# Two groups of heads ahead of the second query block, and a rank 300 ahead for the heads' work, in a two-layer trunk

## The chip, the cores and the metric

The kernel runs on one core of one Trainium2 chip. The core has TensorE (PE in the profile, with its weight loads shown apart as PEld), VectorE (DVE), ScalarE (ACT), GpSimd (POOL) and SyncE (SP), which here issues nearly all DMAs. The metric is device time in microseconds, the median of several runs. One execution of the kernel is profiled.

## The reference

Two layers work on x of 256 rows by 1024 columns in fp32, each as x = x + mixer(rms_norm(x)).

```python
# layer 0 (nsa): 16 query heads in 4 groups g, one key/value head per group
q, kc, vc, ks, vs, kw, vw, gl, z = split(h @ w_in)
q = rope(rms_norm(q));  k_cmp, v_cmp = compress(kc), compress(vc)   # 15 blocks of 32 rows
o = gate0 * attend(q, k_cmp, v_cmp) + gate1 * attend(q, ks, vs) + gate2 * attend(q, kw, vw)
x = x + (o * silu(z)) @ w_out
# layer 1 (swa with sinks): 16 query heads, 2 key/value heads, window of 128
q, k, v, z = split(h @ w_in);  q, k = rope(rms_norm(q)), rope(rms_norm(k))
x = x + (attend(q, k, v, window=128, sink) * silu(z)) @ w_out
```

Every attention needs the queries of its heads, the keys, a masked softmax over at most 256 keys, and at its end the gate silu(z) of its heads.

## The kernel before

The 256 rows are two halves of 128 (h = 0 and 1). The 16 heads are four groups of four, numbered g or u. Every projection works on weights that are loaded in fp32 (`wraw`), copied by ScalarE to a high part (`wh`, line 147) and split by VectorE into a low part (`wl`, line 175), so that each product takes three matmuls. `wraw`, `wh` and `wl` have five buffers each.

Each layer is written as a list of steps. `q0` and `q1` (`queries`, `queries1`) project the queries of heads 0 to 7 and 8 to 15: 48 matmuls 512 columns wide for each, into the two PSUM banks with the tag `acc`. Then `q_prep` applies the rotary factors (VectorE, lines 316 and 317, and GpSimd, line 66), splits the result (`qs`) and transposes it on TensorE into PSUM tiles `ptq` (line 343), which ScalarE copies to `qT`. `z0` to `z3` (`z_gate`) project the gate of one group: 48 matmuls of 256 columns into the one bank `pz`, which VectorE reads out in line 393 (`zt`). `a0` to `a3` (`attend0`, `attend1`) are the heads of one group, for both halves: score matmuls into `s` or `sb` (two banks), scores to `p` on VectorE (line 407), the exponential on ScalarE (line 409), the scaling of `p`, its transposes into `ptp` (line 440) and of the small compressed part into `ptcs` (line 770), the product with the values into `po` (one bank), and `finish_unit`, which multiplies by `zt` and splits the result into `oz` for `out_proj`. `a0` and `a1` need the queries of `q0`, `a2` and `a3` those of `q1`. `out_proj` sums into `pya` (tag `acc`), `pyb` (tag `s`) and, in layer 1, `tail`. `ptn`, `ptk`, `ptq`, `ptp` and `ptcs` share two PSUM banks with the tag `pt`.

The order on each engine is set when the kernel is built, by a scheduler that plays the program through with costs of its own. Among the instructions whose inputs and buffers are ready it takes the one with the lowest rank. An instruction's rank is its place in the written order, and `tc.high_priority(offset=n)` ranks what is inside it n places ahead: 200 for the weight splits (`HP`) and for the read-out of the gate (`HPZ`), 250 for `q_prep` (`HPQ`) and `k_prep` (`HPK`), 100 for the copies out of `ptp` (`HPT`). The heads' work has no offset of its own. Once built, each engine runs its own list in order.

Of the kernel before, what the change touches and what calls it, by code (L numbers as in the profile page):

```python
# [33 lines left out]
EPS = 1e-6  # L34
NEG = -1e30
HP, HPZ, HPS, HPT, HPQ, HPF = 200, 200, 0, 100, 250, 0
HPC, HPK, NWARM2 = 300, 250, 4
RSC, QLO = 'p', 'd'
WPS = ('d', 'd', 'd', 'd', 'd', 'd', 'd', 'd', 'd')
PHASES = (4, 13, 23, 29, 37, 43, 49, 55)  # L40
# [50 lines left out]
def tile_hybrid_trunk(ctx: ExitStack, tc: tile.TileContext, x, positions, norm_gains, a_w_in, a_cmp_pos,  # L91
# [18 lines left out]
    def banks(name, tag="acc"):  # L110
        return [bank(f"{name}{h}", tag) for h in range(2)]
# [66 lines left out]
    def load_w(w, k0, nk, c0, n):  # L178
        return split_w(load_raw(w, k0, nk, c0, n))
# [112 lines left out]
    def proj(acc, hT, h, w, nk, k0):  # L292

        wh, wl = w
        for k in range(nk):
            hh = hT[:, 0, k0 + k, h * 128:(h + 1) * 128]
            hl = hT[:, 1, k0 + k, h * 128:(h + 1) * 128]
            for i, (s, m) in enumerate(((hh, wh), (hh, wl), (hl, wh))):
                mm(acc, s, m[:, k, :], k0 + k == 0 and i == 0, k0 + k == 7 and i == 2)
# [23 lines left out]
    def heads(ap):  # L323
        return ap.rearrange("p (n d) -> p n d", d=HD)
# [458 lines left out]
            finish_unit(po, zt, h, g, oz)  # L783


    for step in 'q0 z0 a0 q1 z1 a1 z2 a2 z3 a3'.split():
        {'q': queries, 'z': zs0, 'a': attend0}[step[0]](int(step[1:]))


    sqs = work.tile([128, 2, 2], F32, name="sqs1", tag="sqs")  # L790
# [25 lines left out]
    def keys1():  # L816
        acc = banks("akv1", "s")
        wk = [load_w(bwi, k0, 4, 1024, 256) for k0 in (0, 4)]
        for kk in range(2):
            for h in range(2):  # L820
                proj(acc[h][:, 0:256], hT, h, wk[kk], 4, 4 * kk)
        k_prep([heads(acc[h][:, 0:128]) for h in range(2)], 2, 5, kt1, (0, 128), r1)
        for h in range(2):
            nc.scalar.activation(v1[:, h], heads(acc[h][:, 128:256]), AF.Copy, scale=r1[:, h:h + 1])
# [40 lines left out]
            pv(po, [(v1[:, b, g, :], transpose_p([ps[i][:, b] for i in range(4)])) for b in range(nb)], True)  # L865
            finish_unit(po, zt, h, u, oz)

    for step in 'q0 k0 z0 a0 q1 z1 a1 z2 a2 z3 a3'.split():
        {'q': queries1, 'k': lambda n: keys1(), 'z': zs1, 'a': attend1}[step[0]](int(step[1:]))
    out_proj(ozs, bwo, xh, None, True)  # L870


# [31 lines left out]
```

## Time and profile before

| | us |
|---|---|
| median of 3 runs | 289.81 |
| lowest and highest run | 289.19, 290.7 |
| the profiled execution, its own time | 289.28 |
| its span, first to last instruction | 287.6 |
| TensorE busy in the span | 272.4 |
| VectorE busy in the span | 217.6 |
| ScalarE busy in the span | 189.4 |
| GpSimd busy in the span | 124.9 |

The span is what the trace covers. The execution's own time is 1.68 us longer, which lies around the span. TensorE's busy time is the time in which at least one matmul is shown as running.

### The profile page before, as it was taken

The numbers are of one execution on the slowest core, as the hardware profiler recorded it, in microseconds if no ns is written. First come the engines' busy times: TensorE is split into PE (matmuls) and PEld (weight loads), VectorE is DVE, ScalarE is ACT, GpSimd is POOL, SyncE is SP. The second block draws the span as 40 slices with busy tenths as digits, with TensorE's granted clock in tenths as the row PEclk, the third lists the DMA queues.
The fourth block names the chain that finished last, engine by engine and source line by source line (L and its number), as shares of the span: only waits on it lengthen the run. The fifth ranks groups of instructions, "written<-read, shape, count | busy, mean of one in ns | idle before, by whom it ended". The sixth has DMA issues, their size and how long they took to land.

```text
span 287.6 us, 5296 instructions
## 1 busy us (share of the span) xinstructions
PE 272.4 (95%) x1780; PEld 232.3 (81%) x1780; DVE 217.6 (76%) x579; ACT 189.4 (66%) x457; POOL 124.9 (43%) x188
## 2 busy tenths in 40 slices
PE   6989999999999799988998999999999799999995
PEld 5858988888989698866776877889989699877874
DVE  3768646999979989969698374859969988784533
ACT  5694991755664758779688474757866949783620
POOL 7489308193552391726252500112694392253200
PEclk9999999999999989999999999999999989999999
DMA  7997845546474334310102345227774423100003
GB/s 224 321 293 244 310 141 146 151 143 166 130 217 146 121 106 140 86 66 13 64 0 76 146 137 159 59 87 217 217 226 148 145 77 106 43 0 0 2 0 146
DMA packets 33114, 37.51 MB, mean 130 GB/s; under 512 B 1680, under 2 KB 21568, under 8 KB 32960
## 3 DMA queue, kind: packets, MB, share of 16 engines
q1 hardware_dynamic: 33088, 37.18, 42.2%
q8 instruction: 14, 0.23, 0.3%
q14 instruction: 12, 0.10, 0.1%
HBM read 36.13 MB, written 1.05 MB: 129 GB/s over the span
## 4 chain that ended last, share of the span: by engine, by line
PE 80%; DVE 12%; ACT 4%; issue 1%; DMA 1%; SPq 0%; ACTq 0%
PE pz L114 13%; PE aqb L114 8%; PE po L114 8%; PE pya L114 7%; PE aq L114 7%; PE pyb L114 7%; PE ptp L440 4%; PE aks L114 4%; DVE wl L175 3%; PE akc L114 3%; PE avw L114 2%; PE s L114 2%; PE sb L114 2%; PE akw L114 2%; PE akv L114 2%; DVE p L407 2%
## 5 line engine op out<-in xcount | busy, mean ns | idle before, releaser
L175 DVE TENSOR_TENSOR wl<-wraw,wh 128x1024 fp32r<-128x1024 f32 (+2 forms) x64 | 80.5, 1261 | 11.2 <-ACT wh L147 10.7
L147 ACT ACTIVATE wh<-wraw 128x1024 fp32r<-128x1024 f32 (+3 forms) x58 | 59.6, 1031 | 26.3 <-issue 5.0
L114 PE MATMUL pz<-hT,wh 128*128 128x256 f32 x256 | 51.4, 296 | 2.0 <-DVE zt L393 2.0
L114 PEld LDWEIGHTS pz<-hT,wh 128*128 128x128 f32 x256 | 42.7, 200 | 2.6 <-DVE zt L393 2.0
L71 POOL TENSOR_SCALAR p<-p,rg 128x256 f32<-128x256 f32 (+1 forms) x48 | 24.1, 522 | 32.1 <-DVE rg L763 16.8
L114 PE MATMUL pz<-hT,wl 128*128 128x256 f32 x128 | 37.5, 293 | 0.0
L66 POOL TENSOR_TENSOR rt<-rt,rt 128x512 f32<-128x512 f32 (+2 forms) x14 | 19.1, 1369 | 42.4 <-DVE rt L317 34.5
L409 ACT ACTIVATE p<-p,nm 128x128 f32<-128x128 f32 (+1 forms) x64 | 28.3, 446 | 3.7 <-DVE nm L407 3.5
L147 ACT ACTIVATE ptsb<-ptp 128x512 f32<-128x512 f32 x36 | 20.5, 586 | 10.4 <-PE ptp L440 10.4
L114 PEld LDWEIGHTS pz<-hT,wl 128*128 128x128 f32 x128 | 25.6, 200 | 0.0
L407 DVE CUSTOM_DVE_ANT_0 p<-s,mask,nrq 128x128 f32<-128x128 f32 (+1 forms) x64 | 24.2, 408 | 0.1
L114 PE MATMUL s<-kt,qT 128*128 128x272 f32 (+1 forms) x96 | 19.8, 306 | 1.8 <-DVE cwide L736 0.7
L114 PE MATMUL aqb<-wh,hT 128*128 128x512 f32 x64 | 21.4, 397 | 0.0
L114 PE MATMUL aq<-wh,hT 128*128 128x512 f32 x64 | 20.9, 395 | 0.0
L71 POOL TENSOR_SCALAR pb<-pb,rg 128x128 f32<-128x128 f32 (+1 forms) x24 | 13.8, 590 | 15.5 <-DVE rg L860 9.8
L407 DVE CUSTOM_DVE_ANT_0 pb<-sb,mask,nsink 128x128 f32<-128x128 f32 (+1 forms) x32 | 13.9, 471 | 5.1 <-PE ptp L440 3.9
L114 PEld LDWEIGHTS s<-kt,qT 128*128 128x128 f32 x96 | 14.4, 190 | 3.5 <-PE s L114 1.2
L273 ACT ACTIVATE hT<-ptn,gT 128x128 fp32r<-128x128 f32 x32 | 10.8, 363 | 9.0 <-PE ptn L267 5.5
L440 PE MATMUL ptp<-identr,p 128*128 128x128 f32 x96 | 14.9, 275 | 1.8 <-ACT ptsb L147 1.8
L409 ACT ACTIVATE pb<-pb,nm 128x128 f32<-128x128 f32 (+1 forms) x32 | 14.2, 447 | 2.6 <-DVE nm L407 2.5
L114 PEld LDWEIGHTS aq<-wh,hT 128*128 128x128 f32 x64 | 12.0, 188 | 2.3
L440 PEld LDWEIGHTS ptp<-identr,p 128*128 128x128 f32 x96 | 11.2, 140 | 3.2 <-ACT ptsb L147 2.6
(246 smaller groups left out, 694.1 us busy)
## 6 DMA issues: line engine op xcount, KB each, us to landing
wraw<-in_a_w_in_dram SPq DMA_DIRECT2D x25, 512.0 KB, 4.0
wraw<-in_b_w_in_dram SPq DMA_DIRECT2D x18, 512.0 KB, 4.3
wraw<-in_a_w_out_dram SPq DMA_DIRECT2D x8, 512.0 KB, 3.6
wraw<-in_b_w_out_dram SPq DMA_DIRECT2D x8, 512.0 KB, 3.7
x<-in_x_dram SPq DMA_DIRECT2D x4, 256.0 KB, 4.5
w<-in_cmp_w_dram SPq DMA_DIRECT2D x1, 1024.0 KB, 4.8
x<-in_x_dram SPq DMA_DIRECT2D x2, 512.0 KB, 3.8
wraw<-in_a_w_in_dram SPq DMA_DIRECT2D x2, 456.0 KB, 6.6
```

Source lines behind the costliest of these rows:

```text
L66: self.eng.tensor_tensor(out, a, b, op=op)
L71: self.eng.tensor_scalar(out, a, s0, s1, op0=op0, op1=op1)
L114: nc.tensor.matmul(o, lhsT=l, rhs=r, start=start, stop=stop)
L147: nc.scalar.activation(dst, src, AF.Copy)
L175: e_.tensor_tensor(wl[:, ks], raw[:, ks], wh[:, ks].bitcast(F32), op=ALU.subtract)
L273: nc.scalar.activation(hi, pt[:, k], AF.Copy, scale=gk)
L407: nc.vector.tensor_tensor_reduce(out=p, in0=s, in1=mk, scale=nr, scalar=floor, op0=ALU.add, op1=ALU.min, accum_out=nm)
L409: nc.scalar.activation(p, p, AF.Exp, scale=-1.0, bias=nm, accum_out=total)
L440: nc.tensor.transpose(pt[:, i], s, ident)
```

## The change

A constant `HPA` of 300 is added. In both layers the step `q1` is written behind `z1 a1` instead of ahead of them, and every step `a` is run inside `tc.high_priority(offset=300)`. The steps themselves stay the same. An `a` step is some 155 instructions in layer 0 and some 85 in layer 1, a `z` step some 60, a `q` step some 100.

```diff
-HPC, HPK, NWARM2 = 300, 250, 4
+HPC, HPK, HPA, NWARM2 = 300, 250, 300, 4
...
-    for step in 'q0 z0 a0 q1 z1 a1 z2 a2 z3 a3'.split():
-        {'q': queries, 'z': zs0, 'a': attend0}[step[0]](int(step[1:]))
+    for step in 'q0 z0 a0 z1 a1 q1 z2 a2 z3 a3'.split():
+        with tc.high_priority(offset=HPA if step[0] == 'a' else 0):
+            {'q': queries, 'z': zs0, 'a': attend0}[step[0]](int(step[1:]))
...
-    for step in 'q0 k0 z0 a0 q1 z1 a1 z2 a2 z3 a3'.split():
-        {'q': queries1, 'k': lambda n: keys1(), 'z': zs1, 'a': attend1}[step[0]](int(step[1:]))
+    for step in 'q0 k0 z0 a0 z1 a1 q1 z2 a2 z3 a3'.split():
+        with tc.high_priority(offset=HPA if step[0] == 'a' else 0):
+            {'q': queries1, 'k': lambda n: keys1(), 'z': zs1, 'a': attend1}[step[0]](int(step[1:]))
```

## Rows read from the trace of the kernel before

**Rows 1.** The page: busy time and share of each engine; chain that ended last.

```profile
PE 272.4 (95%) x1780; PEld 232.3 (81%) x1780; DVE 217.6 (76%) x579; ACT 189.4 (66%) x457; POOL 124.9 (43%) x188
...
PE 80%; DVE 12%; ACT 4%; issue 1%; DMA 1%; SPq 0%; ACTq 0%
```

**Rows 2.** Busy time by stretch: PE, PEld, DVE, ACT, POOL, clock, DMA share, GB/s.

```profile
71.00:118.00 47.00, 44.80 (x317) 41.45 (x317) 42.69 (x120) 31.23 (x80) 23.16 (x23) 0.96 0.50 145
118.00:178.00 60.00, 56.21 (x372) 43.62 (x371) 42.32 (x171) 43.88 (x130) 19.49 (x40) 1.00 0.27 81
```

**Rows 3.** The same columns, for the three stretches in which TensorE loses most.

```profile
96.50:102.70 6.20, 4.21 (x21) 3.79 (x21) 6.13 (x18) 3.84 (x12) 2.67 (x3) 0.72 0.43 137
226.60:232.50 5.90, 3.92 (x20) 3.92 (x21) 5.90 (x19) 4.62 (x17) 4.80 (x5) 0.71 0.29 93
118.00:158.50 40.50, 36.97 (x265) 28.98 (x263) 32.81 (x151) 33.36 (x110) 15.83 (x32) 1.00 0.14 42
```

**Rows 4.** TensorE's waits: total us, times, longest.

```profile
PE pz L114 <- DVE zt L393: 2.0, 2, 1.8
PE sb L114 <- DVE nm L407: 2.0, 1, 2.0
...
PE avw L114 <- ACT wh L147: 1.6, 1, 1.6
```

**Rows 5.** Timeline of TensorE, layer 0 (start, duration, count at the end).

```profile
71.00 0.47 PE L114 MATMUL pz<-hT,wh 128*128 128x256 f32 x2
...
76.82 0.40 PE L114 MATMUL aq<-wh,hT 128*128 128x512 f32 x1
...
83.62 0.73 PE L114 MATMUL s<-kt,qT 128*128 128x272 f32 x4
...
99.33 0.80 PE L114 MATMUL pz<-hT,wh 128*128 128x256 f32 x2 [1.84 <-DVE zt L393]
```

**Rows 6.** Timeline of VectorE around the read-outs of `z0` and `z1`, layer 0.

```profile
76.65 1.23 DVE L175 TENSOR_TENSOR wl<-wraw,wh 128x1024 fp32r<-128x1024 f32 x1 [0.26 <-ACT wh L147]
77.79 0.68 DVE L304 TENSOR_REDUCE qssq<-sq 128x8 f32<-128x512 f32 x1
...
78.99 0.68 DVE L393 TENSOR_TENSOR zt<-pz,rrows 128x512 f32<-128x512 f32 x1
...
97.99 0.68 DVE L256 TENSOR_TENSOR qs<-rt,qs 128x512 fp32r<-128x512 f32 x1
98.59 0.68 DVE L393 TENSOR_TENSOR zt<-pz,rrows 128x512 f32<-128x512 f32 x1
```

**Rows 7.** Timeline of TensorE: transposes of `a0` and `q1`, scores and transpose of `a2`.

```profile
104.96 0.27 PE L770 MATMUL ptcs<-identr,cwide 128*128 128x128 f32 x1
...
122.01 0.60 PE L440 MATMUL ptp<-identr,p 128*128 128x128 f32 x4
...
123.20 0.54 PE L343 MATMUL ptq<-identr,qs 128*128 128x128 f32 x4 [0.35 <-ACT ptsb L147]
...
127.99 0.49 PE L114 MATMUL s<-kt,qT 128*128 128x272 f32 x2
...
140.28 0.27 PE L770 MATMUL ptcs<-identr,cwide 128*128 128x128 f32 x1
```

**Rows 8.** Timeline of layer 1: `q1`, then the wait of the scores.

```profile
206.43 0.40 PE L114 MATMUL aqb<-wh,hT 128*128 128x512 f32 x1
...
218.45 0.39 PE L114 MATMUL pz<-hT,wh 128*128 128x256 f32 x2
...
226.86 0.67 DVE L304 TENSOR_REDUCE qssq<-sq 128x8 f32<-128x512 f32 x1
...
228.58 1.66 PE L114 MATMUL sb<-kt,qTb 128*128 128x128 f32 x8 [2.02 <-DVE nm L407]
```

**Rows 9.** Timeline of TensorE, layer 1: scores of `a2`, then its first transposes.

```profile
246.43 1.11 PE L114 MATMUL sb<-kt,qTb 128*128 128x128 f32 x8
...
256.64 0.60 PE L440 MATMUL ptp<-identr,pb 128*128 128x128 f32 x4
```

## The prediction

> **What bounds the kernel now.** I read the page first. TensorE is busy for 272.4 of the 287.6 us and holds 80% of the chain that ended last; VectorE comes second with 217.6 us [rows 1]. So the end is TensorE's work plus the time in which it stands still or runs slowly, and the change can only touch the latter, since it adds and removes no instruction. Busy time by stretch then shows where that is. From the first gate matmul (71) to the end of layer 0 (178), TensorE is busy for 101.0 of 107 us, and VectorE for 42.7 of the first 47 us but 42.3 of the last 60 [rows 2]: the first part has two full engines, the second one. TensorE's own waits and a finer cut name three places [rows 3, 4].
>
> A: 96.5 to 102.7. TensorE has finished `z1`, the only gate bank still holds it, and `z2` waits 1.84 us for VectorE to read it out (line 393) [rows 5]. VectorE is behind with the split of `q1` (`qs`) [rows 6]. The granted clock of the stretch is 0.72: the matmuls after the wait run for a while at the lower of the two levels. 0.28 of 6.2 us is 1.7 us; with the 1.99 us not busy, A costs 3.7.
>
> B: 226.6 to 232.5, the same in layer 1. Scores wait 2.02 us for VectorE, which has just worked for `q1` (`qssq`) [rows 8]. 1.98 us not busy and 0.29 of 5.9 us: 3.7.
>
> C: 118 to 158.5. The gates and `q1` are used up, and while the heads wait for VectorE and ScalarE only `pya` fills in: 40.50 - 36.97 = 3.5 us [rows 3].
>
> **The change part by part.** *The rank.* By written order `q1` and `z1` stand behind `a0`, and still the weight splits (200 ahead) and `q_prep` (250) pass the heads on VectorE. The trace shows what that costs the heads: from the first score matmul of `a0` to its first `ptcs` 104.96 - 83.62 = 21.3 us pass, for `a2`, which meets fewer splits, 140.28 - 127.99 = 12.3 [rows 5, 7]. With 300 the heads of `a0` and `a1` go first on every engine, so `a0` should reach its transposes some 9 us sooner. That is no gain by itself, as TensorE has other work then. It gains where the fillers run out: with `z2`, `z3` and `pya` left for later, part of C is filled. I take 1.2 of C's 3.5 (bounds: 0, as the two engines are as full as before, and 3.5).
>
> The row of C has the weight loads busy for 28.98 of 40.50 us, 72%, against 41.45 of 47, 88%, from 71 to 118 [rows 2, 3]. The Trainium skill, "Perfetto Trace Analysis", section "Identifying the Most-Contended Engine", says that this share, not the busy time of the matmuls, tells how much room TensorE has left. By it C would hold 40.5 x (1 - 72/88) = 7.4 us in place of 3.5 (an estimate), a third of that 2.5, and the sum below would be 1.3 lower. I stay with 3.5, which the row shows as standing still.
>
> *The place of `q1`, gates.* A `z` step is 76.82 - 71.00 = 5.8 us of TensorE [rows 5]; `q1` is at most 218.45 - 206.43 = 12.0, with the transposes in it [rows 8]. Before, `q1` lies between `z0` and `z1`, so the bank has time to be read; then `z1` and `z2` collide (A). After, `q1` lies between `z1` and `z2`, and `z0` and `z1` are neighbours. In layer 0, `z0` ends at 76.8. VectorE is then inside a weight split and a `qssq` that rank ahead, until 78.4, so the read-out ends near 79.1 [rows 6], and the first weights of `q1` are split only after the two of `z1`. TensorE would stand for some 2 us, less the `ptq` of `q0`. If the clock falls too, the new stall costs 2 + 1.7 = 3.7, all of A; if it doesn't, or if a weight of `q1` is there, 0 to 2. I take a gain of 1.2 out of A (bounds 0 and 3.7). In layer 1 `q1` can start while the bank is read, since its weights are split early, and `z2` finds the bank long free. B should go with its cause, the work for `q1` ahead of the first scores; I take 2.6 (bounds 0 and 3.7), short of all because scores and splits still share VectorE.
>
> *The place of `q1`, transposes.* This is the cost. The transposes of all kinds share two PSUM banks, and the trace shows that these are handed out in written order: `qs` is ready at 98.7, ranked 250 ahead, and yet `ptq` comes at 123.20, right behind the last `ptp` of `a0` at 122.01 [rows 6, 7]. After the change `ptq` must wait for the last `ptp` of `a1`, and only then can `a2` score. So between `a1` and `a2` the heads pause: 127.99 - 123.20 = 4.8 us from the first `ptq` to the scores, and 12.3 from there to the first transpose, 17.1 in all in layer 0 [rows 7]; in layer 1, 4.8 + (256.64 - 246.43) = 15.0 [rows 9]. What hides it is `z2` and `z3`, 11.6 us, besides the products of `a1` and the scores of `a2`. Below, the cost is 0. Above, with those gates alone, or with them spent and the rest in their place, it is 17.1 - 11.6 = 5.5 and 3.4, and 1.7 each if the clock falls: 7.2 and 5.1. I take 0.5 each, near the lower end: `z1` and `q1`, 17.8 us, stand ahead of `z2` in the ring of five weight buffers, so `z2` and `z3` should still be there when `a1` ends.
>
> *Splits behind heads.* The weights of `q1` and the gates are now split after the ready work of the heads. Nothing in the trace shows TensorE short of weights during attention; the nearest row is its wait for a `wh` in the opening, 1.6 us [rows 4], and with 1.7 us of low clock 3.3 a layer. The cover is the ring of five, some 14 us of matmuls at 2.9 each (half a `z` step). I take 0.3 a layer (bounds 0 and 3.3). The DMAs of the weights go through SP in the written order of the loads; `z1`'s two now pass `q1`'s four, none is added, and the DMA share is 0.50 at most in these stretches [rows 2]: 0. The exponentials and copies on ScalarE and the scalings on GpSimd only change order, at 31.2 and 23.2 of 47 us [rows 2]: 0 while VectorE is fuller than both.
>
> Sum: -1.2 - 1.2 - 2.6 + 1.0 + 0.6 = -3.4. Against the profiled execution's 289.28 that is 285.9; the median of the runs shown is 0.53 higher, so 286.4.
>
> **The rivals.** *The pause decides (slower).* `z2` and `z3` are spent before `a1` ends, as TensorE takes whatever is ready whenever the heads wait. Then layer 0's pause costs its 7.2 in place of 0.5: 286.4 + 6.7 = 293.1. For it: stretch C begins, in the kernel before, where all four gates are through, and the last transposes of `a0` come only at 122 [rows 7]. Against it: the heads had no precedence there. It decides once the two pauses together cost more than 5.9 us (the other terms give -4.4, and 1.5 is 0.5%).
>
> *The stalls only move (same).* `z0` and `z1` stall in place of `z1` and `z2`, at the full 3.7, and in layer 1 `z2` and `z3` do so: the -1.2 and -2.6 fall away, 286.4 + 3.8 = 290.2. For it: one gate bank is left and VectorE's total stays. The Trainium skill says the same in "Perfetto Trace Analysis", section "Optimization Strategy": a gap that repeats on the engine that should be full can mean that there are too few buffers. The two waits at the gate bank agree with it; by this rule a new order gives nothing. That the ranks do little, as they only count among instructions ready at the same time, ends here too.
>
> *All three stalls go (much faster).* -3.7 - 3.7 - 3.5 + 1.6 = -9.3: 280.5. For it: the first transposes of `a0` have 9 us to win. Against it: VectorE is 91% busy up to 118.
>
> **How the numbers follow.** Chances: forecast 0.38, all stalls gone 0.10, stalls moved 0.23, pause decides 0.24, and 0.05 that it is slower still, by the pauses of both layers or by weights that come late. I predict the likeliest, 286.4, with 284 to 288.3 as its own range. To leave out no more than 2 in 10 the range reaches into the fast case and past the pause of layer 0: 282.0 to 294.0. Runs of one kernel differ by about 0.5%, which is 1.45 us. Faster: 0.38 + 0.10, and none of the third case, 0.48; same 0.23; slower 0.29.
>
> **What would show it.** In the changed profile the first `ptcs` should come by 97 instead of 104.96 and all `ptq` of `q1` behind `a1`'s last `ptp`. The 1.84 us wait between `z1` and `z2` and the one at 228 should be gone; a wait for line 393 near 77 says that A moved. At the pause I look for `pz` on TensorE between `a1`'s last `ptp` and `a2`'s first. Waits of TensorE there, or for `wh` and `wl`, with a lower clock behind them, would make the prediction wrong; so would a total busy time of TensorE that differs by more than the low clock explains.

## The result, and the profile after

The changed kernel takes 305.69 us (median of 4 runs, 305.0 to 308.9) against 290.25 for the kernel before, timed beside it: a ratio of 1.055 (1.0507 to 1.0593). The prediction was 286.4, with a range up to 294. The span of the profiled execution is 304.3 us against 287.6, so 16.7 us are to be found.

The page after, which answers to [rows 1]: no instruction has been added to TensorE, and its busy time is 8.8 us longer.

```profile
PE 281.2 (92%) x1780; PEld 235.0 (77%) x1780; DVE 218.6 (72%) x579; ACT 190.4 (63%) x457; POOL 123.9 (41%) x188
...
PE 76%; DVE 13%; POOL 4%; DMA 3%; issue 2%; SPq 1%; ACT 1%; POOLq 0%; DVEq 0%
```

Busy time by stretch after, with the columns of [rows 2]. The first four lines are layer 0, from the first gate matmul to the first `aqb` of layer 1; the last four are layer 1.

```profile
71.60:119.00 47.40, 44.99 (x312) 41.38 (x311) 41.16 (x103) 29.91 (x71) 17.95 (x17) 0.96 0.47 137
119.00:143.80 24.80, 21.09 (x140) 15.96 (x139) 13.88 (x57) 16.26 (x45) 12.47 (x22) 0.93 0.19 59
143.80:175.20 31.40, 27.78 (x160) 21.80 (x158) 24.17 (x123) 23.73 (x83) 10.73 (x24) 0.89 0.15 51
175.20:189.80 14.60, 14.60 (x93) 11.18 (x91) 7.93 (x13) 7.88 (x16) 0.00 (x0) 1.00 0.51 144
189.80:231.70 41.90, 41.90 (x268) 37.60 (x266) 32.01 (x51) 26.36 (x49) 17.74 (x20) 1.00 0.53 153
231.70:268.00 36.30, 32.86 (x228) 28.22 (x226) 29.76 (x74) 24.92 (x63) 18.46 (x21) 0.95 0.27 87
268.00:293.90 25.90, 24.54 (x154) 19.68 (x150) 14.85 (x58) 15.75 (x51) 5.24 (x12) 0.93 0.00 1
293.90:304.30 10.40, 6.86 (x39) 5.34 (x38) 3.94 (x8) 0.00 (x0) 0.00 (x0) 1.00 0.28 101
```

Layer 0 lasts 189.8 - 71.6 = 118.2 us, where it had been 179.86 - 71.00 = 108.9: 9.3 more. TensorE stands still for 2.41 + 3.71 + 3.62 = 9.7 us, and the lower clock takes 0.04 x 47.4 + 0.07 x 24.8 + 0.11 x 31.4 = 7.1. Before, the same sums over 71 to 178 are 6.0 and 1.9 [rows 2]. So 3.7 us more are idle time and 5.2 more low clock, together 8.9 of the 9.3. Layer 1 with the tail grows by 6.8. There the three lossy lines hold 8.3 us of idle time and 3.6 of low clock, against 5.2 and 2.2 in layer 1 of the kernel before:

```profile
179.86:287.56 107.70, 102.49 (x677) 89.21 (x675) 79.98 (x190) 67.96 (x163) 41.29 (x53) 0.98 0.31 98
```

That is some 4.5 of the 6.8 us; the rest lies in neither. The reader should note the second line after the change: between 119 and 143.8 VectorE is busy for 13.88 of 24.8 us, 56%, where stretch C of before had it at 32.81 of 40.5, 81% [rows 3]. Neither engine is full there.

TensorE's timeline in layer 0, which answers to [rows 5, 7]:

```profile
99.88 0.27 PE L770 MATMUL ptcs<-identr,cwide 128*128 128x128 f32 x1
...
119.21 0.28 PE L114 MATMUL pz<-hT,wl 128*128 128x256 f32 x1
...
138.38 1.14 PE L440 MATMUL ptp<-identr,p 128*128 128x128 f32 x8 [0.58 <-ACT ptsb L147]
...
140.76 0.79 PE L343 MATMUL ptq<-identr,qs 128*128 128x128 f32 x8
...
143.82 0.75 PE L114 MATMUL s<-kt,qT 128*128 128x272 f32 x4
...
149.86 0.82 PE L114 MATMUL s<-kt,qT 128*128 128x272 f32 x4 [0.37 <-DVE nm L407]
151.94 1.22 PE L114 MATMUL s<-kt,qT 128*128 128x272 f32 x4 [1.27 <-DVE nm L407]
153.56 1.34 PE L114 MATMUL s<-kt,qT 128*128 128x272 f32 x4 [0.39 <-DVE rg L763]
154.70 0.42 PE L770 MATMUL ptcs<-identr,cwide 128*128 128x128 f32 x1
```

The first `ptcs` of `a0` comes 5.1 us earlier than before (99.88 for 104.96). The last gate matmul of `z3` runs at 119.21. The last `ptp` of `a1` starts at 138.38, and only behind it `ptq`, at 140.76; 13.9 us later, at 154.70, come the first transposes of `a2`. In the kernel before they came at 140.28 [rows 7]. No `pz` is left for the 15.2 us between 139.5 and 154.7. In layer 1 the same happens: `z3` is over at 255.7, the last `ptp` of `a1` are in the row at 264.52, and `ptq` follows at 266.77:

```profile
255.38 0.28 PE L114 MATMUL pz<-hT,wl 128*128 128x256 f32 x1
...
264.52 1.03 PE L440 MATMUL ptp<-identr,pb 128*128 128x128 f32 x8
...
266.77 0.46 PE L343 MATMUL ptq<-identr,qs 128*128 128x128 f32 x4
...
274.64 1.05 PE L440 MATMUL ptp<-identr,pb 128*128 128x128 f32 x4
277.03 0.74 PE L114 MATMUL sb<-kt,qTb 128*128 128x256 f32 x4 [1.34 <-DVE nm L407]
```

TensorE's waits, which answer to [rows 4]:

```profile
PE s L114 <- DVE nm L407: 5.2, 8, 1.3
PE avw L114 <- ACT wh L147: 2.1, 1, 2.1
...
PE sb L114 <- DVE nm L407: 1.3, 1, 1.3
```

The wait at the gate bank (1.84 us in A) has gone, as forecast, but not what it cost: the first of the eight lines above has 2.41 us of idle time and a clock of 0.96, where 71 to 118 had 2.20 and 0.96 before [rows 2]. In its place the scores at 107.99 and 109.50 wait 0.79 and 1.02 us for VectorE. In all of layer 0 scores (`s`) wait for line 407 eight times, 5.2 us together, where before it was once, for 0.6 us.

### The profile page after: what moved, and what is told of

Its sections match the earlier page's. It is cut to its first block, busy times and chain, and to the rows that moved or that the text cites. A ratio compares the mean times of both kernels' runs of the same rounds, so it can differ in the third digit from the quotient of the medians.

```text
span 304.3 us, 5297 instructions
## 1 busy us (share of the span) xinstructions
PE 281.2 (92%) x1780; PEld 235.0 (77%) x1780; DVE 218.6 (72%) x579; ACT 190.4 (63%) x457; POOL 123.9 (41%) x188
## 4 chain that ended last, share of the span: by engine, by line
PE 76%; DVE 13%; POOL 4%; DMA 3%; issue 2%; SPq 1%; ACT 1%; POOLq 0%; DVEq 0%
PE pz L114 13%; PE aq L114 7%; PE aqb L114 7%; PE pya L114 7%; PE pyb L114 7%; PE po L114 6%; PE ptp L440 4%; DVE wl L175 4%; PE s L114 4%; PE aks L114 4%; DMA posi<-in_positions_dram 3%; PE avw L114 2%; DVE p L407 2%; PE akv L114 2%; PE akw L114 2%
## 5 line engine op out<-in xcount | busy, mean ns | idle before, releaser
L114 PE MATMUL pz<-hT,wh 128*128 128x256 f32 x256 | 54.0, 297 | 0.1
L114 PEld LDWEIGHTS pz<-hT,wh 128*128 128x128 f32 x256 | 43.9, 202 | 0.8 <-DVE zt L393 0.3
L71 POOL TENSOR_SCALAR p<-p,rg 128x256 f32<-128x256 f32 (+1 forms) x48 | 22.8, 495 | 38.3 <-DVE cm L757 15.9
L114 PE MATMUL s<-kt,qT 128*128 128x272 f32 (+1 forms) x96 | 22.5, 341 | 6.8 <-DVE nm L407 5.2
L114 PEld LDWEIGHTS s<-kt,qT 128*128 128x128 f32 x96 | 16.7, 215 | 11.4 <-PE s L114 3.2
L114 PE MATMUL aqb<-wh,hT 128*128 128x512 f32 x64 | 22.8, 398 | 0.0
L71 POOL TENSOR_SCALAR pb<-pb,rg 128x128 f32<-128x128 f32 (+1 forms) x24 | 11.4, 492 | 24.5 <-DVE rg L861 21.3
L440 PE MATMUL ptp<-identr,p 128*128 128x128 f32 x96 | 16.4, 298 | 1.4 <-ACT ptsb L147 0.6
L422 DVE SCALAR_TENSOR_TENSOR of<-po,zt 128x256 f32<-128x256 f32 x14 | 5.9, 421 | 13.6 <-PE po L114 13.6
L440 PEld LDWEIGHTS ptp<-identr,p 128*128 128x128 f32 x96 | 12.6, 154 | 2.7 <-ACT ptsb L147 0.8
```

What stands on the lines that cost most here:

```text
L71: self.eng.tensor_scalar(out, a, s0, s1, op0=op0, op1=op1)
L114: nc.tensor.matmul(o, lhsT=l, rhs=r, start=start, stop=stop)
L422: nc.vector.scalar_tensor_tensor(of, po, 0.5, zt[:, 2 * g4:2 * g4 + 2, h * 128:(h + 1) * 128], op0=ALU.mult, op1=ALU.mult)
L440: nc.tensor.transpose(pt[:, i], s, ident)
```

## The experiments

Three theories were set against each other. *Place*: `ptq` of `q1` must wait for the last `ptp` of `a1`, since both use the two `pt` banks, handed out in written order. *Heads ahead*: the rank of 300 starves weights and gates. *Lost counter*: leaving a `tc.high_priority` block sets the counter of places back to where it stood on entry. While the changed kernel is built, every `q` and `z` step of layer 0 starts at place 357 and every one of layer 1 at 484 (the `a` steps 300 lower); in the kernel before they start at 357, 409, 459, 603 and so on to 1239 for `out_proj`. So even an offset of 0 is no empty wrapper: the first instructions of all steps tie, and the steps mix. The statement ahead of the prediction that a rank is the place in the written order is incomplete by this.

| run | order of steps | offset of 300 on `a` | places | banks of `ptq` of `q1` | median, us | ratio to before |
|---|---|---|---|---|---|---|
| after | new | yes | lost | pt | 305.69 | 1.055 (1.0507 to 1.0593) |
| e1 | new | no | kept | pt | 303.68 | 1.0461 (1.0418 to 1.0504) |
| e2 | old | yes | lost | pt | 297.53 | 1.0263 (1.0229 to 1.0298) |
| e3 | old | no | lost | pt | 301.15 | 1.039 (1.0338 to 1.0442) |
| e4 | new | yes | kept | pt | 305.98 | 1.0527 (1.047 to 1.0584) |
| e5 | old | yes | kept | pt | 290.53 | 1.0012 (0.9981 to 1.0042) |
| e6 | new | no | kept | acc | 292.52 | 1.0088 (1.0051 to 1.0125) |
| e7 | new | yes | kept | acc | 288.03 | 0.993 (0.9904 to 0.9957) |
| e8 | old | no | kept | acc | 286.81 | 0.9888 (0.9853 to 0.9923) |
| e9 | new | yes | lost | acc | 291.09 | 1.0044 (1.002 to 1.0069) |
| e10 | old | yes | kept | acc | 286.61 | 0.9902 (0.9862 to 0.9941) |
| e11 | `q1` between `z1` and `a1` | no | kept | pt | 290.6 | 1.0039 (1.0009 to 1.0068) |

The kernel before took 289.65 to 289.7 us beside e1 to e11. Differences in us are those of the medians; a ratio, which has its interval, can differ from their quotient by up to 0.4%. Each run left one profiled execution. Of the two loops over the steps a diff shows that of layer 0; that of layer 1 has the same edit.

**e1, the order alone.** The kernel before, with

```diff
-    for step in 'q0 z0 a0 q1 z1 a1 z2 a2 z3 a3'.split():
+    for step in 'q0 z0 a0 z1 a1 q1 z2 a2 z3 a3'.split():
         {'q': queries, 'z': zs0, 'a': attend0}[step[0]](int(step[1:]))
```

> q1 is written behind z1 a1 in both layers, and nothing is ranked anew. Three theories stand for the 15 us that the change costs. Place: the transposes of q1 must wait for the last transposes of a1, whatever the ranks, and the heads pause; then this kernel is slow too, at 298 to 306 us. Heads ahead: the rank of 300 starves the weights and the fillers; then this one stays within 287 to 292. Lost counter: leaving a ranked block sets the place counter back to where it stood, so that in the changed kernel all steps of the loop share one place and nothing is kept as a filler; this one has no such block, and lies within 286 to 293, with pz on TensorE between the last ptp of a1 and the first ptcs of a2.

It costs 14.0 us, nearly all of the loss, with no rank touched. TensorE's timeline shows the same chain as after:

```profile
136.61 1.03 PE L440 MATMUL ptp<-identr,p 128*128 128x128 f32 x8
137.90 1.03 PE L343 MATMUL ptq<-identr,qs 128*128 128x128 f32 x8 [0.25 <-ACT ptsb L147]
...
148.97 3.59 PE L114 MATMUL s<-kt,qT 128*128 128x256 f32 x10 [0.96 <-DVE nm L407]
152.35 0.41 PE L770 MATMUL ptcs<-identr,cwide 128*128 128x128 f32 x1
```

A reader who goes by TensorE's waits alone misses this. The one in front of `ptq` is 0.25 us; that its operand had lain ready since 106.8, for 31 us, stands only in VectorE's timeline:

```profile
106.15 0.62 DVE L256 TENSOR_TENSOR qs<-rt,qs 128x512 fp32r<-128x512 f32 x1
```

One has to compare the place of `ptq` among the other tiles of its banks.

**e2, the ranked blocks with the old order.** The changed kernel, with

```diff
-    for step in 'q0 z0 a0 z1 a1 q1 z2 a2 z3 a3'.split():
+    for step in 'q0 z0 a0 q1 z1 a1 z2 a2 z3 a3'.split():
         with tc.high_priority(offset=HPA if step[0] == 'a' else 0):
```

> The old order of steps, with the ranked blocks of the change around every step. Place: the pause between a1 and a2 is gone, 288 to 292 us. Heads ahead and lost counter alike: most of the loss remains, 296 to 306.

7.9 us are lost here too, by something that is not the place of `q1`.

**e3, the old order in blocks with an offset of 0.** As e2, with

```diff
-HPC, HPK, HPA, NWARM2 = 300, 250, 300, 4
+HPC, HPK, HPA, NWARM2 = 300, 250, 0, 4
```

> The old order of steps, every step inside a block with an offset of 0: the heads are not ranked ahead at all, and only the counter of places is set back after each step. Place and heads ahead: no change, 288 to 292 us. Lost counter: 295 to 306 us, with gates through before 120 us and low clock behind waits for line 407 after that.

The lost counter alone costs 11.5 us in the old order; the heads' 300 places on top of it (e2) give some of that back. Part of what was expected in the trace did not show: the gates are through by 115.8 us, but no low clock follows in layer 0 (granted clock 1.00 from 115.8 to 185.2). Two rows of TensorE show where much of it goes:

```profile
185.22 0.40 PE L114 MATMUL aqb<-wh,hT 128*128 128x512 f32 x1
...
236.49 0.74 PE L114 MATMUL sb<-kt,qTb 128*128 128x128 f32 x5
```

From the first projection of layer 1 to its first scores 51.3 us pass. In the kernel before the same two rows are 41.2 us apart:

```profile
179.86 0.40 PE L114 MATMUL aqb<-wh,hT 128*128 128x512 f32 x1
...
221.01 1.08 PE L114 MATMUL sb<-kt,qTb 128*128 128x128 f32 x8
```

With `q0`, `k0`, `z0` and `q1` mixed, the first heads get their inputs 10.1 us later. The first of e3's rows comes 5.4 us late, 1.5 of them from the opening of this execution; behind its second row the heads make some of the delay good.

**e4, the change as the prediction took it: places kept.** The changed kernel, with

```diff
+        at, ahead = tc.cur_priority, HPA if step[0] == 'a' else 0
-        with tc.high_priority(offset=HPA if step[0] == 'a' else 0):
+        with tc.high_priority(offset=ahead):
             {'q': queries, 'z': zs0, 'a': attend0}[step[0]](int(step[1:]))
+            done = tc.cur_priority
+        tc.cur_priority = done + ahead
```

> The new order, with every step a ranked 300 ahead, but the counter of places goes on behind each step as if it had been written without the block, which is what the prediction took the change to be. Place: 298 to 306 us. Heads ahead: 296 to 306. Lost counter: what the prediction forecast, 283 to 290, with pz on TensorE at the pause between a1 and a2.

*Lost counter* falls as the cause of the change's loss: with the places kept it is as slow. The last gate matmul is over even sooner, and `ptq` comes behind the last `ptp` again:

```profile
115.79 0.28 PE L114 MATMUL pz<-hT,wl 128*128 128x256 f32 x1
...
139.41 1.04 PE L440 MATMUL ptp<-identr,p 128*128 128x128 f32 x8
140.70 0.53 PE L343 MATMUL ptq<-identr,qs 128*128 128x128 f32 x4 [0.25 <-ACT ptsb L147]
```

**e5, the rank alone, places kept.** The blocks of e4 with the old order.

> The old order of steps, every step a ranked 300 ahead, the counter of places going on as if the block were not there. This is the rank of the change alone, without its order and without the lost places. If heads ranked ahead are harmless, as the prediction took it (a gain of 1.2 us, 0.6 lost on late splits), 287 to 291 us. If heads ahead starve the weights and the fillers, 294 to 302.

No change that can be measured, so *heads ahead* falls. Beside the new order the same rank adds 2.3 us (e4 against e1), with intervals that overlap.

**e6, e7 and e8, other banks for the transposes of `q1`.** The edit in `q_prep`, laid on e1, on e4 and on the kernel before:

```diff
-                    pt = ps_t.tile([128, 4, 128], F32R, name="ptq", tag="pt")
+                    pt = (ps_s if h0 else ps_t).tile([128, 4, 128], F32R, name="ptq", tag="acc" if h0 else "pt")
```

> The new order with nothing ranked anew, and the transposes of q1 put into the two banks with the tag acc, which the projection of q1 has just left, in place of the two that the heads transpose into. So they no longer wait for the last transposes of a1. If that wait makes the pause, the scores of a2 come before a1 has ended, and most of the 14 us of the order come back: 288 to 294 us. If the order costs by what it does to the gates and splits, 300 to 305 remain.

> The same move of the transposes, with the new order and the heads ranked 300 ahead with places kept. If the wait for the banks is the whole of the loss, 285 to 292 us, and what the prediction promised for the stalls at the gate bank and before the scores can show. If ranked heads cost by themselves, 296 or more.

> The control: the kernel before, with the transposes of q1 in the acc banks and nothing else changed. There they wait for a0's last transposes alone, and all of a1 fills the time, so little should come of it: 287 to 291 us by the bank theory. If it gains as much as the same move under the new order (some 10 us, so 278 to 282), the banks cost the kernel before just as much and don't explain the difference.

The banks take 11.2 us off e1 and 18.0 off e4, but 2.9 off the kernel before. So the wait for the `pt` banks makes most of the pause, and it is there for the order that was changed: *place* stands. It is not the whole of what the order costs. With the banks freed the new order still takes 5.7 us more than the old one (e6 against e8). The stretch behind the gates, which are over at 115.3 in e6, shows where, e6 first and e8 below:

```profile
118.00:130.00 12.00, 9.62 (x40) 7.40 (x42) 9.71 (x45) 8.30 (x29) 7.02 (x14) 0.57 0.15 44
118.00:130.00 12.00, 11.59 (x82) 8.68 (x82) 10.60 (x52) 10.65 (x36) 4.34 (x8) 1.00 0.16 46
```

The scores of `a2` begin at 132.57 in e6, and until then only `a0`, `a1` and `pya` are left for TensorE: 2.4 us idle and 5.2 of low clock, against 0.4 and none. With the banks freed the heads' rank, of no effect in e5, gives the new order 4.5 us. The control gained a little more than the banks were expected to give. Its stretches A and B show why:

```profile
96.50:102.70 6.20, 4.83 (x44) 4.63 (x44) 6.20 (x18) 5.97 (x16) 1.47 (x4) 1.00 0.51 168
226.60:232.50 5.90, 5.13 (x44) 4.89 (x44) 5.87 (x20) 5.90 (x19) 5.08 (x5) 1.00 0.35 107
```

`ptq` of `q1` now runs at 98 to 103 and 225 to 229 and fills just these gaps: TensorE is busy for 4.83 and 5.13 us in place of 4.21 and 3.92, at the full clock in place of 0.72 and 0.71 [rows 3]. (This execution reached layer 0 1.5 us later than the one before and layer 1 0.6 us sooner; windows moved along by that give the same busy times and clock.)

**e9, the same edit on the changed kernel.**

> The changed kernel as it is, with one thing altered: the transposes of q1 go into the acc banks, so that a2 need not wait for the last transposes of a1. If that wait is nearly all of the 15.4 us, 287 to 293 us. If the places lost at each block cost as much by themselves as they did in the old order (8 us with the heads ahead), 295 to 300.

Other banks for one tile bring back 305.69 - 291.09 = 14.6 us: the kernel is then 0.4% slower than before. Layer 0 by TensorE's timeline and a stretch:

```profile
106.29 0.87 PE L343 MATMUL ptq<-identr,qs 128*128 128x128 f32 x8 [1.24 <-DVE qs L256]
...
139.89 0.27 PE L770 MATMUL ptcs<-identr,cwide 128*128 128x128 f32 x1
```

```profile
119.00:160.00 41.00, 36.91 (x252) 28.64 (x253) 34.68 (x173) 33.72 (x118) 19.07 (x35) 1.00 0.15 45
```

and the same stretch of the changed kernel:

```profile
119.00:160.00 41.00, 34.44 (x205) 26.19 (x203) 28.66 (x139) 29.86 (x98) 14.58 (x28) 0.88 0.16 49
```

`ptq` is 34 us earlier and the first transposes of `a2` come at 139.89 for 154.70. In the same 41 us VectorE does 6.0 us more work and TensorE 47 more matmuls, at a clock of 1.00 for 0.88. Against e7 (ratio 0.993), the lost places cost the remaining 1.1%. From 119 to 143.8, which is the second of the eight lines of the changed kernel, e9 has

```profile
119.00:143.80 24.80, 21.51 (x150) 16.55 (x151) 20.21 (x102) 20.18 (x71) 12.75 (x23) 1.00 0.15 43
```

VectorE is busy for 20.21 us in place of 13.88 and the clock is 1.00 in place of 0.93, but TensorE's idle time is nearly the same, 3.29 for 3.71.

**e10, rank with places kept and freed banks, old order.**

> The old order, every step a ranked 300 ahead with places kept, and the transposes of q1 in the acc banks. If ranked heads help once the banks don't hold them up (as between the two runs with the new order, where they gave 4.5 us), 282 to 286 us. If the new order was what made the rank useful, 286 to 289.

286.61 us, the same as e8. Once the banks are free the rank helps only the new order, and even with it that order stays 1.4 us behind (e7 against e10). e8 and e10 are the two fastest, about 1% below the kernel before, and neither has the new order.

**e11, `q1` behind `z1` but ahead of `a1`.** The kernel before, with

```diff
-    for step in 'q0 z0 a0 q1 z1 a1 z2 a2 z3 a3'.split():
+    for step in 'q0 z0 a0 z1 q1 a1 z2 a2 z3 a3'.split():
```

> q1 is written behind z1 but still ahead of a1, nothing is ranked anew and the banks are as before. The transposes of q1 then come ahead of those of a1, as before, and no pause is made. If the place ahead of or behind a1 is what counts, 287 to 293 us. If it is q1 behind z1, with the gate bank read out between two gates, 297 to 304.

0.4% slower than before, where e1, with `q1` one step further back, is 4.6% slower. So passing `a1` costs 13.1 us (12.2 by the ratios) and passing `z1` about 1. Its stretches, against [rows 2], in windows that begin 2 us later because this execution reached layer 0 at 72.99 in place of 71.00:

```profile
73.00:120.00 47.00, 44.38 (x319) 40.67 (x318) 43.94 (x112) 32.15 (x76) 22.68 (x19) 1.00 0.48 147
120.00:180.00 60.00, 56.47 (x365) 43.75 (x363) 42.02 (x182) 44.11 (x134) 21.20 (x44) 0.97 0.26 80
```

The low clock of stall A has gone (1.00 for 0.96) and is paid back behind 120 (0.97 for 1.00); TensorE's idle time is 6.2 us over both lines, where it was 6.0.

## Why the prediction was wrong

**The step that failed** is the pause between `a1` and `a2`. The prediction named it, with its cause, and the runs bear the cause out (e1, e6, e9, e11). It then priced it at 0.5 us a layer, since "`z2` and `z3` should still be there when `a1` ends". What the runs show in its place is 13.1 us for both layers (e1 against e11). The two gates never were there: `z3` ended by 121.2 us in layer 0 of every run, with the heads ranked ahead or not, places kept or lost, and the last `ptp` of `a1` came at 137 to 141 where the order was new and the banks were old. In layer 1 of the changed kernel the two times are 255.7 and some 265. The reason given, that `z1` and `q1` stand ahead of `z2` in the weight ring, says in which order the gates come, not how late. TensorE had 71 to 118 nearly full in the kernel before [rows 2], with the gates as its fillers, and it went on to take them while the heads of `a0` and `a1` waited for VectorE. Kept back, they would have been missing there instead; that was argued from these rows and not tried. The rival "the pause decides" said this and was given 0.24.

**Its size** was low in the rival too: it put the full price, 7.2 us, on layer 0 alone. With the upper bound of layer 1, 5.1, it would have been 12.3. Passing `a1` measured 13.1 us, and other banks gave the changed kernel 14.6 back (after against e9), though the control shows that 2.9 of such a gain can be had in the old order too (e8). Even the upper bounds took the 11.6 us of the two gates off, as if other work stood in for them once they were spent. Two more things were left out. The low clock was counted once a layer, at 1.7 us; in layer 0 it took 5.2 more than before, in the lines of 0.93 and 0.89. And the pause thins out what lies ahead of it: with `a2` shut out, the rest of `a0` and `a1` are the only heads from 119 on, and VectorE is busy for 56% of that line, where e9 has 81%. The 3.71 us of idle time in that line are mostly not the pause's, as e9 has 3.29 there. The spent gates are also what is left when the banks are freed: e6 loses its 5.7 us behind them.

**Point by point.** The rank (-1.2, and +0.6 for late splits) comes to nothing with places kept (e5, 0.9981 to 1.0042): right within its bounds. The first `ptcs` came at 99.88, not by 97. The place of `q1` behind `z1` (-1.2 and -2.6) was worth a slight loss (e11): the wait and the low clock of A went and came back elsewhere, much as the rival "the stalls only move" had it. Its place for them, the gate bank ahead of `z3` in layer 1, holds only 0.21 us in e11, but 2.75 us in e1 and e4. `ptq` behind the last `ptp`, and waits with a low clock at the pause, were named as signs, and both are in the trace. The lost counter was not in the prediction at all. It costs the old order 7.9 to 11.5 us (e2, e3), and the change itself about 1.1% once the banks are free (e7 against e9), but nothing visible while the pause decides (after against e4).

The prediction cited the Trainium skill, "Perfetto Trace Analysis", section "Optimization Strategy", for a gap that too few buffers make. The runs agree in kind, though the banks that were short were the two of `pt` and not the gate bank: other banks repaid 14.6 us, where no rank or order did. The Trainium skill, "Perfetto Trace Analysis", section "Matmul Optimizations", asks that all eight PSUM banks be used. Here the two `acc` banks lay idle in layer 0 from 96.5, when the projection of `q1` was last read, to 118.0, when `out_proj` began, and e8 gains 1.1% by using them. No run here shows the estimate from the weight loads' share, that stretch C holds 7.4 us: none was built for C alone, and none gained more than 1.1%.

## What to carry to other kernels

When a step is moved in the written order, list every ring of buffers that it shares with what it passes: the tile that is handed out later waits for the last one handed out earlier, however high its rank, and giving it another bank is the test. Don't count on filler work for a later gap while the engine that would do it already has gaps before. When a block sets a rank, look at where the counter stands behind the block, since a wrapper with an offset of 0 cost 4% here.

## What the runs showed of the hardware

Between two kernels a mean granted clock is a poor guide to the time. The profiled execution of e9 has 1.00 over its whole span and took 290.89 us, that of e7 has 0.987 and took 288.10: the one loses its time in idle TensorE (271.0 us busy of 289.2), the other is busy for 273.2 of 286.4. Between executions of one kernel it is a good guide. The kernel before, timed 46 times beside e1 to e11, took 287.9 to 288.7 us where its mean clock was 0.994, 289.1 to 290.2 at 0.987 or 0.988, and 290.6 to 292.0 at 0.981 or 0.982.

In stretch A of before one wait of 1.84 us went with 1.7 us of low clock [rows 3, 5]. In the changed kernel four waits of scores between 148.5 and 153.6, of 0.33 to 1.27 us and 2.4 us together, went with a granted clock of 0.50, the lower of the two levels, from 151.4 to 158.2: 3.4 us.
